# A hybrid mLSTM and attention trunk on one core: halo sums on ScalarE, a ratio with two scalar factors, residual rows loaded as their bank begins

## The chip, the cores and the metric

The kernel runs on one core of one Trainium2 chip. The core has five engines that run side by side, each through its own list of instructions in a fixed order: TensorE (PE in the profile; its weight loads are PEld), VectorE (DVE), ScalarE (ACT), GpSimd (POOL) and SyncE (SP), which here issues all DMAs. They wait for each other by semaphores. The metric is the device time of one execution in microseconds (us), lower is better.

## The reference

Two layers over 2048 rows of width 1024, float32. Each layer normalises the rows, projects them, and splits the columns between two groups of four heads.

```python
h = rmsnorm(x, norm_w)
proj = jnp.einsum('bsd,de->bse', h, w_in)
mq, mk, mv, mi, mf, mz, aq, ak, av, az = jnp.split(proj, idx, axis=-1)
qk = jax.nn.silu(causal_conv(jnp.concatenate([mq, mk], -1), conv_w, conv_b))
...
hm = mlstm_chunkwise(to_heads(mq_c), to_heads(mk_c), to_heads(mv), mi + i_bias, mf + f_bias)
ym = (rmsnorm(hm) + m_skip * mq_c) * jax.nn.silu(mz)
...
ha = diff_attention(qa, ka, av, lam)      # (softmax(q1 k1) - lam * softmax(q2 k2)) v, block-causal
ya = rmsnorm(ha) * (1.0 - lambda_init) * jax.nn.silu(az)
y = jnp.einsum('bse,ed->bsd', jnp.concatenate([ym, ya], -1), w_out)
return x + y
```

`causal_conv` is a depthwise convolution with four taps over time: each output row is a weighted sum of this row and the three before it, plus a bias. Behind the two layers stands one more RMSNorm.

## The kernel before

The rows are cut into four tiles of 512 (t = 0 to 3), each layer goes through its tiles in order, and each tile through four units (u = 0 to 3), one for each pair of an mLSTM head and an attention head: 32 units in all. In a unit TensorE makes six projections of 128 columns (mq, mk, the two gates, and two halves of the rotary q and k) and the value projection, each as products of a high and a low part of both sides; the high parts of the weights are made by ScalarE (`wh`, line 194), the low parts by GpSimd (`wl`, line 196). Beside them run the attention scores (tiles `sc`, `p`), the transposes of the probabilities (`tpa`), which ScalarE copies out as `ath` (line 801) and VectorE completes as `atl` (line 802), the products with the values (`pv`), and the mLSTM recurrence (`ml`).

The order on TensorE is laid down by a planner in the main loop: each task has a time in a list `sched`, tasks of the projections ("P") are chained one behind another, and the side streams ("A" scores, "V" values, "M" mLSTM) are pinned at places of that chain. On the other engines a scheduler of the framework sorts the instructions by the times of its own model of the run, and each engine then works through its list in order. A tile that is allocated anew waits until the last reader of the buffer's earlier content is done; a DMA that waits holds up what stands behind it in SyncE's queue.

The places that the change touches:

- `proj_conv` (line 397), called twice in each unit, for mq and mk, so 64 times. When the projection has landed in a PSUM bank (`mm`), `post` makes the convolution in the SBUF tile `cacc`. Line 406: ScalarE writes tap 3 and the bias. Lines 410 and 412: for each of the other three taps VectorE adds the shifted bank (509 to 511 columns) and, by one small instruction of 1, 2 or 3 columns, what comes from the three last columns of the tile before, the `halo`. Line 414: ScalarE copies the last three columns of the bank into `halo`, for the tile that follows. Lines 394 and 395: the SiLU, a tanh on ScalarE (`th`) and a product on VectorE.
- `ratio` inside `scores` (line 682), 128 times: the two sums of exponentials of a block of 128 queries, `zz`, become the factor by which the second probability map is added to the first. Line 692 takes a reciprocal, line 693 multiplies it by `zz` and by `nl` (minus lambda), a column of 128 equal numbers, as a `scalar_tensor_tensor` with two tensor operands. Line 699 (`chunk`) uses the factor.
- `outproj` (line 880), the output projection, runs in two passes for each tile. The first (`hh` = 0, units 0 and 1) adds the residual rows of the layer's input and stores the sum in DRAM (`xp`); the second (`hh` = 1, units 2 and 3) runs in unit 1 of the next tile, adds the rows of `xp` and stores to `xo`. A pass has eight banks of 256 rows by 256 columns. Lines 915 and 916 load the residual rows `xr` when the bank's last product is issued, line 921 adds, line 925 squares for the next norm (second pass only), line 926 stores. The tag `xr` has two buffers, the tag `x` four. Tag `x` also serves the rows that `prep_t` (line 250) and `prep_x` (line 226) read for the next tile, and the rows of `final` (line 968). Of the last tile the sums stay in SBUF (`rows`), and its second pass loads nothing.

Of the kernel before, what the change touches and what calls it, by code (L numbers as in the profile page):

```python
# [19 lines left out]
P = 128  # L20
# [32 lines left out]
def trunk_kernel(ctx, tc, x, w_ch, w_v0, w_v, w_o, nw, cw, cb, gb, mnw, msk, anw, lam,  # L53
# [83 lines left out]
    def params(l):  # L137
        pr = par[l]
        for nm, src, w in (("cw", cw[l], 32), ("cb", cb[l], 8),
                           ("mnw", mnw[l], NH), ("msk", msk[l], NH), ("anw", anw[l], 1)):  # L140
            t_ = cp.tile([P, w], F32, tag=f"{nm}{l}", name=f"{nm}{l}")
            SY.dma_start(t_, src)
            pr[nm] = t_
        t_ = cp.tile([P, 8], F32, tag=f"gb{l}", name=f"gb{l}")
        SY.dma_start(t_, gb[l].partition_broadcast(P))
        pr["gb"] = t_
        lt = st([P, 4, 64], "tmp", name="lam")
        SY.dma_start(lt, lam[l].partition_broadcast(P))
        lam_init = 0.8 - 0.6 * math.exp(-0.3 * l)
        lp = st([P, 2, 64], "tmp", name="lp")  # L150
        behind(V.tensor_tensor(lp[:, 0], lt[:, 0], lt[:, 1], op=ALU.mult))
        behind(V.tensor_tensor(lp[:, 1], lt[:, 2], lt[:, 3], op=ALU.mult))
        ls = cp.tile([P, 4], F32, tag=f"ls{l}", name=f"ls{l}")
        V.tensor_reduce(out=ls[:, 0:2], in_=lp, axis=AX.X, op=ALU.add)
        A.activation(ls[:, 2:4], ls[:, 0:2], AF.Exp)
        nl = cp.tile([P, 1], F32, tag=f"nl{l}", name=f"nl{l}")

        V.tensor_tensor(nl, ls[:, 3:4], ls[:, 2:3], op=ALU.subtract)
        V.tensor_scalar(out=nl, in0=nl, scalar1=-lam_init, scalar2=None, op0=ALU.add)
        pr["nl"] = nl  # L160

        behind(V.tensor_scalar(out=pr["anw"], in0=pr["anw"], scalar1=(1.0 - lam_init), scalar2=0.5,
                               op0=ALU.mult, op1=ALU.mult))
        behind(V.tensor_scalar(out=pr["mnw"], in0=pr["mnw"], scalar1=0.5, scalar2=None, op0=ALU.mult))
        behind(V.tensor_scalar(out=pr["msk"], in0=pr["msk"], scalar1=0.25, scalar2=None, op0=ALU.mult))

        for h in range(NH):
            hq = cp.tile([P, 2, 3], F32, tag=f"halo{l}{h}", name=f"halo{l}{h}")
            G.memset(hq, 0.0)
            pr["halo"].append(hq)  # L170
        mc = cp.tile([1, NH], F32, tag=f"mc{l}", name=f"mc{l}")
        G.memset(mc, 0.0)
        pr["mc"] = mc
# [220 lines left out]
        A.activation(th, src, AF.Tanh, scale=0.5)  # L394
        V.scalar_tensor_tensor(out=dst, in0=th, scalar=1.0, in1=src, op0=ALU.add, op1=ALU.mult)

    def proj_conv(l, u, qk, H, X):

        pr = par[l]

        def post(ps):
            halo = pr["halo"][u]
            ch = qk * NH + u
            w = lambda j: pr["cw"][:, ch * 4 + j:ch * 4 + j + 1]
            acc = st([P, T], "tmp", name="cacc")
            A.activation(acc, ps, AF.Identity, scale=w(3), bias=pr["cb"][:, ch:ch + 1])  # L406
            for j in (2, 1, 0):

                d = 3 - j
                V.scalar_tensor_tensor(out=acc[:, d:], in0=ps[:, 0:T - d], scalar=w(j), in1=acc[:, d:],  # L410
                                       op0=ALU.mult, op1=ALU.add)
                V.scalar_tensor_tensor(out=acc[:, 0:d], in0=halo[:, qk, j:3], scalar=w(j), in1=acc[:, 0:d],
                                       op0=ALU.mult, op1=ALU.add)
            A.activation(halo[:, qk], ps[:, T - 3:T], AF.Copy)
            nm = "mq" if qk == 0 else "mk"
            X[nm] = st([P, T], nm)
            silu2(X[nm], acc)

        return proj_ch(l, u, qk, H, post)
# [244 lines left out]
    def scores(l, t, u, X, pair):  # L664
# [19 lines left out]
        def ratio(qi, cq, r=None):  # L684
            zz = X["zz"]
            qb = 2 * pair + qi
            z_ = V.tensor_reduce(out=zz[:, qb], in_=cq["zc"][:, :, 0:t + 1], axis=AX.X, op=ALU.add)
            if r is not None:
                after(z_, r)

            s_ = cq["s"] = sm(1, "s12")
            V.reciprocal(s_, zz[:, qb, 1:2])
            V.scalar_tensor_tensor(out=s_, in0=s_, scalar=zz[:, qb, 0:1], in1=pr["nl"], op0=ALU.mult, op1=ALU.mult)
            X["aa", pair].append(cq["pc"][0])

        def chunk(qi, cq, kt, r=None):
# [183 lines left out]
    def outproj(l, t, hh, Xs, es=(0, 1, 2, 3), R=None, halves=(0, 1), c=None):  # L880
# [5 lines left out]
        def task(dq, i, e, lo):  # L886
            def f():
                if e == es[0] and not lo:
                    c["ps"] = pst("mm", [P, 2, 256])
                if (dq, e // 2) not in c["w"]:  # L890
                    c["w"][dq, e // 2] = load_w(w_o[l, hh, dq, e // 2], 512)
                j = e % 2
# [11 lines left out]
                if lo and e == es[-1]:  # L904
# [7 lines left out]
                    if R is not None and hh == 1:  # L912
                        V.tensor_tensor(R[i, dq], c["ps"], R[i, dq], op=ALU.add)  # L913
                        return
                    xr = st([P, 2, 256], "xr")
                    SY.dma_start(xr, src[rows, cs].rearrange("(b p) c -> p b c", p=P))
                    if R is not None:
                        R[i, dq] = st([P, 2, 256], "hth", name="rows")
                        V.tensor_tensor(R[i, dq], c["ps"], xr, op=ALU.add)
# [121 lines left out]
    for k in range(-1, N + 1):  # L1041
# [22 lines left out]
        if cur:  # L1064
# [5 lines left out]
            att += total(q0) + total(q1) + 1.1 * len(v0)  # L1070
            if u == 2 and s < last:
                at(xc, lambda s=s: rs0.__setitem__(s + 1, prep_x((s + 1) // n_t, (s + 1) % n_t)))
            segs.append((0.0, proj_conv(l, u, 0, H, X) + proj_conv(l, u, 1, H, X)))
            if u == 1 and s > 0:
                pl, pt_ = divmod(s - 1, n_t)
                segs.append((fin_t[k - 2] + 6.0, outproj(pl, pt_, 1, Xs[k - 3:k - 1])))
# [173 lines left out]
```

## Time and profile before

| what | value |
|---|---|
| times of the runs | 2815.98, 2825.23 and 2827.08 us (median 2825.23 us) |
| the profiled execution's own time | 2837.46 us |
| its span, first to last instruction | 2835.5 us |
| TensorE busy | 2671.6 us (94%) |
| VectorE, ScalarE, GpSimd busy | 1862.6, 1649.2, 1433.4 us |

The span is what the profiler saw of one execution; the difference of 1.96 us to its own time lies around the first and the last instruction. Busy time is the time in which an engine had an instruction in work; an engine that waits for a semaphore isn't busy. Since TensorE is busy for 94% of the span, its idle time, and what ended each piece of it, is what to look for; an instruction on another engine matters by what TensorE waits for behind it. A wait is put down to the instruction whose semaphore came last. The clock column (PEclk) is the granted TensorE clock as a share of its full speed; 0.50 is 1.2 GHz and 1.00 is 2.4 GHz.

### The profile page before, as it was taken

The numbers are of one execution on the slowest core, as the hardware profiler recorded it, in microseconds if no ns is written. First come the engines' busy times: TensorE is split into PE (matmuls) and PEld (weight loads), VectorE is DVE, ScalarE is ACT, GpSimd is POOL, SyncE is SP. The second block draws the span as 40 slices with busy tenths as digits, with TensorE's granted clock in tenths as the row PEclk, the third lists the DMA queues.
The fourth block names the chain that finished last, engine by engine and source line by source line (L and its number), as shares of the span: only waits on it lengthen the run. The fifth ranks groups of instructions, "written<-read, shape, count | busy, mean of one in ns | idle before, by whom it ended". The sixth has DMA issues, their size and how long they took to land. (4 is left out here: it accounts for less than half of the span.)

```text
span 2835.5 us, 49306 instructions
## 1 busy us (share of the span) xinstructions
PE 2671.6 (94%) x16692; PEld 2371.3 (84%) x16692; DVE 1862.6 (66%) x4890; ACT 1649.2 (58%) x4413; POOL 1433.4 (51%) x1190
## 2 busy tenths in 40 slices
PE   7999899989999999999999999999999999998997
PEld 6898788888888888888888888888888888887887
DVE  5556565775767767567755566567667676776776
ACT  5555465565656556665555555555566555665665
POOL 5565655545454354344445656555554544445425
PEclk9999999999999999999999999999999999999999
DMA  6645555464544544434445455654557444464333
GB/s 203 174 131 157 169 167 149 140 200 150 167 144 128 173 127 127 131 108 139 147 142 177 141 169 154 198 188 137 159 145 231 141 138 154 116 192 145 100 104 119
DMA packets 249789, 431.02 MB, mean 152 GB/s; under 512 B 30400, under 2 KB 106688, under 8 KB 249536
## 3 DMA queue, kind: packets, MB, share of 16 engines
q1 hardware_dynamic: 249536, 427.87, 50.0%
q8 instruction: 132, 2.16, 0.3%
q14 instruction: 121, 0.99, 0.1%
HBM read 314.38 MB, written 63.05 MB: 133 GB/s over the span
## 5 line engine op out<-in xcount | busy, mean ns | idle before, releaser
L196 POOL TENSOR_TENSOR wl<-wr,wh 128x512 fp32r<-128x512 f32 (+1 forms) x684 | 907.6, 1332 | 1070.4 <-PE mm L106 461.7
L194 ACT ACTIVATE wh<-wr 128x512 fp32r<-128x512 f32 (+1 forms) x684 | 428.1, 628 | 414.2 <-PE mm L106 223.5
L106 PE MATMUL mm<-hth,wh 128*128 128x512 f32 x1536 | 619.7, 403 | 0.4 <-ACT vaug L347 0.4
L106 PE MATMUL mm<-htl,wh 128*128 128x512 f32 x1536 | 610.3, 397 | 0.0
L735 DVE TENSOR_SCALAR_CACHE_REDUCE p<-sc 128x512 f32<-128x512 f32 (+3 forms) x640 | 384.7, 606 | 141.7 <-PE sc L106 116.8
L679 ACT ACTIVATE p<-p,nm 128x512 f32<-128x512 f32 (+3 forms) x640 | 413.8, 649 | 97.6 <-DVE nm L675 86.9
L106 PE MATMUL mm<-hth,wl 128*128 128x512 f32 x1536 | 438.8, 400 | 0.0
L106 PEld LDWEIGHTS mm<-hth,wh 128*128 128x128 f32 x1536 | 291.2, 190 | 60.2 <-ACT vaug L347 1.2
L106 PEld LDWEIGHTS mm<-htl,wh 128*128 128x128 f32 x1536 | 291.0, 189 | 56.8
L106 PEld LDWEIGHTS mm<-hth,wl 128*128 128x128 f32 x1536 | 284.1, 190 | 60.2
L699 DVE SCALAR_TENSOR_TENSOR p<-p,s 128x512 f32<-128x512 f32 (+2 forms) x320 | 284.9, 901 | 1.8
L106 PE MATMUL mm<-wh,hth 128*128 128x256 f32 (+1 forms) x1024 | 268.2, 291 | 16.9 <-DVE gt L349 6.0
L802 DVE TENSOR_TENSOR atl<-tpa,ath 128x512 fp32r<-128x512 f32 x288 | 197.1, 684 | 120.4 <-ACT ath L801 119.4
L106 PE MATMUL mm<-wh,htl 128*128 128x256 f32 (+1 forms) x1024 | 264.2, 288 | 0.0
L106 PE MATMUL sc<-kp,q 128*128 128x512 f32 x768 | 246.2, 406 | 5.5 <-DVE p L735 5.4
L801 ACT ACTIVATE ath<-tpa 128x512 fp32r<-128x512 f32 x288 | 170.1, 591 | 139.7 <-PE tpa L109 134.2
L106 PEld LDWEIGHTS mm<-wh,hth 128*128 128x128 f32 x1024 | 198.4, 194 | 22.3 <-issue 9.0
L106 PEld LDWEIGHTS mm<-wh,htl 128*128 128x128 f32 x1024 | 198.3, 194 | 2.5
L109 PE MATMUL tpa<-ident,p 128*128 128x128 f32 x1088 | 186.1, 276 | 15.1 <-DVE tpa L794 8.7
L410 DVE SCALAR_TENSOR_TENSOR cacc<-mm,cw,cacc 128x511 f32<-128x511 f32 (+2 forms) x192 | 141.6, 737 | 66.5 <-ACT cacc L406 64.7
L106 PE MATMUL pv<-ath,vp 128*128 128x256 f32 x768 | 178.9, 287 | 1.1 <-ACT ath L801 1.1
L106 PE MATMUL mm<-wl,hth 128*128 128x256 f32 (+1 forms) x1024 | 166.8, 292 | 0.4 <-POOL wl L196 0.4
(211 smaller groups left out, 5685.1 us busy)
## 6 DMA issues: line engine op xcount, KB each, us to landing
wr<-in_w_ch_dram SPq DMA_DIRECT2D x384, 256.0 KB, 2.7
wr<-in_w_o_dram SPq DMA_DIRECT2D x140, 256.0 KB, 2.9
q<-ab SPq DMA_DIRECT2D x256, 128.0 KB, 2.4
vp<-vd SPq DMA_DIRECT2D x48, 512.0 KB, 4.6
wr<-in_w_v_dram SPq DMA_DIRECT2D x96, 256.0 KB, 3.7
kp<-kd SPq DMA_DIRECT2D x48, 512.0 KB, 3.8
wr<-in_w_v_dram SPq DMA_DIRECT2D x64, 264.0 KB, 3.0
kc<-ab SPq DMA_DIRECT2D x256, 64.0 KB, 2.0
```

What stands on the lines that cost most here:

```text
L106: pin(PE.matmul(o, l, r, start=start, stop=stop, skip_group_check=True))
L109: pin(PE.transpose(o, i, ident[:n, :n]))
L194: A.activation(wh[:, :n], wr[:, :n], AF.Copy)
L196: G.tensor_tensor(wl[:, :n], wr[:, :n], f32(wh[:, :n]), op=ALU.subtract)
L410: V.scalar_tensor_tensor(out=acc[:, d:], in0=ps[:, 0:T - d], scalar=w(j), in1=acc[:, d:], op0=ALU.mult, op1=ALU.add)
L679: A.activation(pp[:, :w], pp[:, :w], AF.Exp, bias=nm[:, m:m + 1], accum_out=zc[:, m, kt:kt + 1])
L699: d_ = V.scalar_tensor_tensor(out=pc[0][kt][:, :w], in0=pc[1][kt][:, :w], scalar=cq["s"][:, 0:1], in1=pc[0][kt][:, :w], op0=ALU.mult, op1= ...
L735: ev = V.tensor_scalar(out=pp[:, :w], in0=ps[:, :w], scalar1=0.125, scalar2=None, op0=ALU.mult, op1=ALU.max, accum_out=c["mx"][:, m, kt:kt ...
L801: A.activation(ah, p2, AF.Copy)
L802: lo_ = V.tensor_tensor(al, p2, f32(ah), op=ALU.subtract)
```

## The change

Three edits. (1) The halo tile no longer holds three columns of the bank but the finished sums that the three first rows of the next tile need: it has a second slot, so that one can be read while the other is written (`was` and `left`), and one tile per unit serves both layers. VectorE's three small instructions per convolution become one addition of three columns, left out in the first tile of a layer; ScalarE's copy becomes one scaled copy and three instructions of one column each that add to it, left out in the last tile. (2) Line 693 of before becomes a `tensor_scalar` whose two factors are columns read as scalars. (3) The load of the residual rows is called as the bank's first product is issued, and in the second pass it takes the tag `x`.

```diff
-            hq = cp.tile([P, 2, 3], F32, tag=f"halo{l}{h}", name=f"halo{l}{h}")
-            G.memset(hq, 0.0)
+            hq = cp.tile([P, 2, 2, 3], F32, tag=f"halo{h}", name=f"halo{l}{h}")
...
-    def proj_conv(l, u, qk, H, X):
+    def proj_conv(l, t, u, qk, H, X):
...
         def post(ps):
-            halo = pr["halo"][u]
             ch = qk * NH + u
             w = lambda j: pr["cw"][:, ch * 4 + j:ch * 4 + j + 1]
+            was, left = [pr["halo"][u][:, qk, i] for i in (t % 2, 1 - t % 2)]
...
                 V.scalar_tensor_tensor(out=acc[:, d:], in0=ps[:, 0:T - d], scalar=w(j), in1=acc[:, d:],
                                        op0=ALU.mult, op1=ALU.add)
-                V.scalar_tensor_tensor(out=acc[:, 0:d], in0=halo[:, qk, j:3], scalar=w(j), in1=acc[:, 0:d],
-                                       op0=ALU.mult, op1=ALU.add)
-            A.activation(halo[:, qk], ps[:, T - 3:T], AF.Copy)
+            if t > 0:
+                V.tensor_tensor(acc[:, 0:3], acc[:, 0:3], was, op=ALU.add)
+            if t < n_t - 1:
+
+                e = ps[:, T - 3:T]
+                A.activation(left, e, AF.Copy, scale=w(0))
+                for j in (1, 2):
+                    for i in range(3 - j):
+                        A.activation(left[:, i:i + 1], e[:, i + j:i + j + 1], AF.Identity, scale=w(j), bias=left[:, i:i + 1])
...
-            V.scalar_tensor_tensor(out=s_, in0=s_, scalar=zz[:, qb, 0:1], in1=pr["nl"], op0=ALU.mult, op1=ALU.mult)
+            V.tensor_scalar(out=s_, in0=s_, scalar1=zz[:, qb, 0:1], scalar2=pr["nl"][:, 0:1], op0=ALU.mult, op1=ALU.mult)
...
                 if e == es[0] and not lo:
                     c["ps"] = pst("mm", [P, 2, 256])
+                    if not (es == (3,) or R is not None and hh == 1):
+                        rows, cs = slice(i * 256, (i + 1) * 256), slice(dq * 256, (dq + 1) * 256)
+                        c["xr"] = st([P, 2, 256], "xr" if hh == 0 else "x")
+                        SY.dma_start(c["xr"], src[rows, cs].rearrange("(b p) c -> p b c", p=P))
...
-                    xr = st([P, 2, 256], "xr")
-                    SY.dma_start(xr, src[rows, cs].rearrange("(b p) c -> p b c", p=P))
+                    xr = c["xr"]
```

In the changed program VectorE has 48 of the three-column additions (now line 412) where it had 192 halo instructions, and ScalarE 48 scaled copies (now line 416) and 144 one-column instructions (now line 419) where it had 64 copies.

The first place is ScalarE's list at one convolution (layer 0, second tile, unit 1, mq). `halo_293` before and `halo_292` now are the halo tile of that unit, `cacc` the convolution, `th` the tanh of it, `ath` the transposed probabilities. Before:

```order
L406 ACTIVATE cacc<-mm,cb_267,cw_265 128x512
L451 ACTIVATE ab<-t_4648 128x512
L596 ACTIVATE hs<-ml 128x129
L814 ACTIVATE ot<-pv 128x256
L600 ACTIVATE mjunk,mss<-hs 128x128
L801 ACTIVATE ath<-tpa 128x512
L194 ACTIVATE wh<-wr 128x512
L414 ACTIVATE halo_293<-mm 128x3
L394 ACTIVATE th<-cacc 128x512
```

Now:

```order
L405 ACTIVATE cacc<-mm,cb_267,cw_265 128x512
L591 ACTIVATE kw<-ml,cols 128x128
L456 ACTIVATE ab<-t_4642 128x512
L819 ACTIVATE ot<-pv 128x256
L806 ACTIVATE ath<-tpa 128x512
L193 ACTIVATE wh<-wr 128x512
L416 ACTIVATE halo_292<-mm,cw_265 128x3
L393 ACTIVATE th<-cacc 128x512
L419 ACTIVATE halo_292<-mm,halo_292,cw_265 128x1 x3
```

The scaled copy stands where the copy stood, in front of the tanh; it waits for VectorE's third tap, where the copy waited for the last halo instruction. The three one-column instructions stand behind the tanh, the first and the third with a wait for a write by ScalarE itself.

The second place is VectorE's list at the same convolution. `atl` is the completed transposed probabilities, `C` the mLSTM state, `den` and `st` the mLSTM's own. Before:

```order
L410 SCALAR_TENSOR_TENSOR cacc<-mm,cw_265,cacc 128x511
L412 SCALAR_TENSOR_TENSOR cacc<-halo_293,cw_265,cacc 128x1
L410 SCALAR_TENSOR_TENSOR cacc<-mm,cw_265,cacc 128x510
L412 SCALAR_TENSOR_TENSOR cacc<-halo_293,cw_265,cacc 128x2
L410 SCALAR_TENSOR_TENSOR cacc<-mm,cw_265,cacc 128x509
L597 SCALAR_TENSOR_TENSOR C_559<-C_559,dec,ml 128x129
L412 SCALAR_TENSOR_TENSOR cacc<-halo_293,cw_265,cacc 128x3
L607 SCALAR_TENSOR_TENSOR den<-hs 128x4
```

Now:

```order
L807 TENSOR_TENSOR atl<-tpa,ath 128x512
L409 SCALAR_TENSOR_TENSOR cacc<-mm,cw_265,cacc 128x511
L589 TENSOR_TENSOR st<-ml,bc 128x128
L409 SCALAR_TENSOR_TENSOR cacc<-mm,cw_265,cacc 128x510
L409 SCALAR_TENSOR_TENSOR cacc<-mm,cw_265,cacc 128x509
L412 TENSOR_TENSOR cacc<-cacc,halo_292 128x3
L807 TENSOR_TENSOR atl<-tpa,ath 128x512
```

Of six instructions of a convolution four are left, and the addition of the halo is the last of them.

The third place is SyncE's queue in the second pass of layer 0's first tile. `xp` is the DRAM tensor that the first pass wrote, `xo` the one that the second writes, `wr` the raw weights. Before:

```order
L926 DMA xo_0_89<-xr 128x2x256
L192 DMA wr<-in_w_o_dram 128x512
L460 DMA kd_1_1_4681<-kc 128x1024
L192 DMA wr<-in_w_o_dram 128x512
L916 DMA xr<-xp_0_81 128x2x256
L658 DMA vp<-vd_3_0_2549 128x1024
L926 DMA xo_0_89<-xr 128x2x256
L192 DMA wr<-in_w_o_dram 128x512 x2
L916 DMA xr<-xp_0_81 128x2x256
```

Now:

```order
L934 DMA xo_0_89<-x 128x2x256
L191 DMA wr<-in_w_o_dram 128x512
L465 DMA kd_1_1_4675<-kc 128x1024
L191 DMA wr<-in_w_o_dram 128x512
L898 DMA x<-xp_0_81 128x2x256
L563 DMA bc<-bw_1_4056 128x2x512
L663 DMA vp<-vd_3_0_2541 128x1024
L934 DMA xo_0_89<-x 128x2x256
L191 DMA wr<-in_w_o_dram 128x512 x2
```

The row `x<-xp` in the second piece is the load of the fifth bank, where the row `xr<-xp` at the same distance behind the first store was the load of the third: the loads of four banks, not of two, now stand ahead of the pass, already in the first pass's stretch of the queue. In the first pass the loads stand where they stood, each behind the store of two banks earlier, since the tag there still has two buffers.

## Rows read from the trace of the kernel before

**Rows 1.** Page, busy time of each engine and share of the span

```profile
PE 2671.6 (94%) x16692; PEld 2371.3 (84%) x16692; DVE 1862.6 (66%) x4890; ACT 1649.2 (58%) x4413; POOL 1433.4 (51%) x1190
```

**Rows 2.** Windows: stretch, length; PE, PEld, DVE, ACT, POOL busy; PEclk; DMA

```profile
32.00:2800.00 2768.00, 2634.27 (x16449) 2338.28 (x16450) 1827.25 (x4807) 1611.24 (x4314) 1396.44 (x1133) 0.98 0.50 151
```

**Rows 3.** Waits of TensorE, 32 to 2800 us: waiter, waited for; us, times, longest

```profile
PE pv L106 <- DVE atl L802: 35.2, 34, 4.6
PE ml L109 <- ACT hs L617: 10.5, 7, 4.7
PE sc L106 <- DVE p L735: 10.2, 15, 1.2
PE ml L106 <- ACT kw L586: 10.1, 9, 2.1
PE pv L106 <- ACT ath L801: 8.6, 9, 2.7
...
PE mm L106 <- DVE xr L921: 6.2, 5, 2.9
...
PE tpa L109 <- DVE s L692: 5.3, 2, 3.2
```

**Rows 4.** VectorE by form: count, busy us, mean ns, idle before

```profile
L693 DVE SCALAR_TENSOR_TENSOR s<-s,zz,nl 128x1 f32<-128x1 f32 x128 | 45.8, 358 | 2.1
...
L412 DVE SCALAR_TENSOR_TENSOR cacc<-halo,cw,cacc 128x1 f32<-128x1 f32 x64 | 38.4, 600 | 0.0
...
L412 DVE SCALAR_TENSOR_TENSOR cacc<-halo,cw,cacc 128x2 f32<-128x2 f32 x64 | 32.8, 512 | 0.0
...
L412 DVE SCALAR_TENSOR_TENSOR cacc<-halo,cw,cacc 128x3 f32<-128x3 f32 x64 | 28.1, 438 | 0.0
...
L835 DVE TENSOR_TENSOR ar<-zz 128x4 f32<-128x4 f32 x31 | 10.7, 346 | 0.0
```

**Rows 5.** Lines 693 and 212: shortest, median, longest duration in ns

```profile
L693 DVE SCALAR_TENSOR_TENSOR s<-s,zz,nl x128: 124/220/1325, 80.8 to 2775.1; 128x1 f32<-128x1 f32 x128
L212 DVE TENSOR_SCALAR xrs<-xrs x16: 145/154/156, 5.6 to 628.6; 128x1 f32<-128x1 f32 x16
```

**Rows 6.** Timeline around one convolution: start, duration [idle before, released by]

```profile
1102.14 1.42 DVE L412 SCALAR_TENSOR_TENSOR cacc<-halo,cw,cacc 128x1 f32<-128x1 f32 x1
1102.24 1.30 POOL L196 TENSOR_TENSOR wl<-wr,wh 128x512 fp32r<-128x512 f32 x1
...
1104.26 0.57 ACT L801 ACTIVATE ath<-tpa 128x512 fp32r<-128x512 f32 x1
...
1105.43 1.26 POOL L196 TENSOR_TENSOR wl<-wr,wh 128x512 fp32r<-128x512 f32 x1 [1.88 <-ACT halo L414]
1105.44 1.26 DVE L693 SCALAR_TENSOR_TENSOR s<-s,zz,nl 128x1 f32<-128x1 f32 x1
...
1106.63 0.68 DVE L802 TENSOR_TENSOR atl<-tpa,ath 128x512 fp32r<-128x512 f32 x1
...
1107.36 0.58 PE L106 MATMUL pv<-atl,vc 128*128 128x256 f32 x1 [2.09 <-DVE atl L802]
```

**Rows 7.** Windows of TensorE behind that wait

```profile
1109.00:1111.00 2.00, 2.00 (x7) 0.50 0.63 143
```

**Rows 8.** Windows: 42 stretches of 8 us and more behind line 406, summed

```profile
sum 527.00, PE 506.68 PEld 424.55 DVE 428.74 ACT 291.63 POOL 326.82; mean PE 12.06 PEld 10.11 DVE 10.21 ACT 6.94 POOL 7.78
```

**Rows 9.** ScalarE by form, as rows 4

```profile
L406 ACT ACTIVATE cacc<-mm,cb,cw 128x512 f32<-128x512 f32 x64 | 49.1, 767 | 7.6 <-PE mm L106 7.4
...
L394 ACT ACTIVATE th<-mm 128x512 f32<-128x512 f32 x64 | 37.8, 590 | 14.5 <-PE mm L106 14.3
...
L414 ACT ACTIVATE halo<-mm 128x3 f32<-128x3 f32 x64 | 10.8, 169 | 85.0 <-DVE cacc L412 84.8
```

**Rows 10.** Waits of all engines, as rows 3

```profile
DVE xr L921 <- DMA xr<-xp: 28.1, 12, 4.4
```

**Rows 11.** Windows: the seven stretches of the second pass, summed

```profile
sum 255.00, PE 247.92 PEld 236.63 DVE 173.31 ACT 170.48 POOL 88.26; mean PE 35.42 PEld 33.80 DVE 24.76 ACT 24.35 POOL 12.61
```

More of the change, by code (lines that the diff above doesn't have):

```diff
@@ L1072, in trunk_kernel @@
                 at(xc, lambda s=s: rs0.__setitem__(s + 1, prep_x((s + 1) // n_t, (s + 1) % n_t)))
-            segs.append((0.0, proj_conv(l, u, 0, H, X) + proj_conv(l, u, 1, H, X)))
+            segs.append((0.0, proj_conv(l, t, u, 0, H, X) + proj_conv(l, t, u, 1, H, X)))
             if u == 1 and s > 0:
```

## The prediction

> **What bounds the kernel now.** I read the page's busy times first. TensorE works for 2671.6 of 2835.5 us, the next engine, VectorE, for 1862.6 [rows 1]. So only TensorE's idle time can be won or lost. The windows say where it is: between 32 and 2800 us TensorE is busy for 2634.27 of 2768.00 us, which leaves 133.7 us idle [rows 2]; the rest lies at the two ends, which the change hardly touches. The waits say what ends it. The largest group, 35.2 us in 34 pieces, is TensorE standing before `pv` until VectorE has made `atl`; 10.2 us are waits for `p`, 5.3 us for the instruction just ahead of the ratio, and 10.5, 10.1 and 8.6 us are waits for ScalarE (`hs`, `kw`, `ath`) [rows 3]. No single wait is large (76 pieces in these six groups), and each is there because VectorE or ScalarE was still working through its list. A change on those engines is worth what it takes off these waits, not the time that it takes off the engine.
>
> One more thing makes a wait dearer than it looks. Behind the wait that ended at 1107.36 us [rows 6], TensorE ran from 1109 to 1111 us without a gap at a granted clock of 0.50, the 1.2 GHz level [rows 7]: those 2 us hold 1 us of work at full speed.
>
> **Edit 1, VectorE's side.** It removes 192 small instructions: 38.4 + 32.8 + 28.1 = 99.3 us [rows 4], 1.55 us for each of 64 convolutions. It adds 48 additions of 128x3. The nearest row is an addition of 128x4 from two SBUF tensors, 346 ns on average [rows 4]: 48 x 0.346 = 16.6 us. From below I bound it by a one-source instruction of one column, 0.15 us [rows 5], so 7 us, from above by the dearest halo form, 0.60 us [rows 4], so 29 us. VectorE is relieved by about 83 us (70 to 92).
>
> Why a 128x1 instruction takes 600 ns is seen in the timeline: one took 1.42 us, while GpSimd's `wl` ran from 1102.24 to 1103.54 us, and line 693 took 1.26 us while the next `wl` ran for 1.26 us from 1105.43 us [rows 6]. Both have two tensor inputs in SBUF. Behind them stood `atl`, started at 1106.63 us though its input `ath` was done at 1104.83 us, and behind `atl` TensorE for 2.09 us. With the edits that list is shorter by 1.42 and two times some 0.2 us of halo work and by 1.1 us of ratio, less 0.35 us for the addition: `atl` could start when `ath` is there, 1.8 us earlier, and of the 2.09 us some 0.3 would be left. This is one of the best places, not a typical one.
>
> What it is worth over all: the stretches behind the 64 convolutions (42 of them, since the two of a unit often touch) are 527.00 us long and TensorE is busy in them for 506.68 us [rows 8]. So 20.3 us of idle time can go at most, and part of it ends on ScalarE. I take half, 10 us. What is late next in those stretches is `ath` on ScalarE, or TensorE itself.
>
> **Edit 1, ScalarE's side.** 64 copies of 169 ns go (10.8 us). A scale and a bias read from columns cost 767 - 590 = 177 ns, by the same shape with and without them [rows 9]; one of them I take at 88 ns. The scaled copy then takes 0.26 us and each one-column instruction 0.35 us: 0.26 + 3 x 0.35 = 1.31 us, 48 times, 63 us. ScalarE's work grows by 52 us (22 us if the columns cost nothing, 85 us if an instruction takes 0.5 us, because each adds to what the one before has written; no row shows that wait). Against this stands the wait of the old copy for VectorE's last halo instruction, 84.8 us [rows 9]; the new one waits for the third tap only, 1.55 us earlier, and 16 convolutions have none. So ScalarE comes out about even, but its work stands closer to `ath` and `kw`, for which TensorE waits already [rows 3]. I charge 2 us (0 to 24, the upper end worked out below).
>
> **Edit 2.** Line 693 takes 358 ns on average, 124 at the shortest and 1325 at the longest [rows 4, 5]. A `tensor_scalar` of the same 128x1 took 145 to 156 ns in all its 16 instances [rows 5]. By that row 128 x (358 - 152) = 26 us of VectorE's time go. The other bound is nothing, if the new form is held up by GpSimd as the old one was. On the path: 51 waits of TensorE end at `atl`, `p` or `s` [rows 3]; if a ratio stood ahead of every one, 0.2 us each, 10 us. It stands ahead of a minority, so I take 3 us.
>
> Here the Trainium skill speaks against the edit. Its page "SBUF — State Buffer", section "Who interferes with whom", says that a VectorE instruction with two SBUF inputs contends with a GpSimd instruction that reads SBUF, and that `tensor_scalar` can contend too when it runs in a two-port mode; whoever starts first holds the shared ports for its whole instruction. The first half agrees with the 1.42 and 1.26 us above [rows 6]. By the second half the edit would save nothing and the sum below would be 3 us smaller; the 16 instances of the one-column `tensor_scalar` without a long one [rows 5] speak against it here.
>
> **Edit 3.** In the first pass nothing moves: the loads already stand as early as two buffers allow. In the second pass VectorE waited 28.1 us, 12 times, for the loads [rows 10], which themselves wait in SyncE's queue for the stores of two banks earlier. With four buffers VectorE's wait should go. But in the seven stretches of the second pass TensorE is busy for 247.92 of 255.00 us [rows 11], so 7.1 us is all there is, and in both passes together it stood for 6.2 us behind the addition of the rows [rows 3]. I take 1 us (0 to 7). The loads of `prep_x` for the next tile, which share the tag, now come behind the second pass; they have a unit's time until they are used, so I cost them at nothing. If that cover is gone, the transposes of the next tile wait.
>
> **The sum.** 10 + 3 + 1 - 2 = 12 us of waits. With some of the longer waits a stretch at the 1.2 GHz level goes too; I take three of them at 1 us [rows 7]. Total 15 us. The profiled execution's own time is 2837.46 us, so its like would be 2822.5 us; that execution lay 12.2 us above the median of the runs, so I predict 2837.5 - 15 - 12.2 = 2810 us, 0.5% under the 2825.2 us. Its own range, from 7 to 25 us of gain, is 2800 to 2818 us.
>
> **Rivals.** (a) The relief is hidden. TensorE's order is fixed, and where one engine is earlier, another ends the same wait: behind `atl` stands `ath`, behind that TensorE's own transposes. For it speaks that the convolution stretches are idle for 3.9% (20.3 of 527), hardly less tight than the 4.8% overall (133.7 of 2768); against it the list of [rows 6], where nothing else was late. Gain 3 us: 2822 us (2815 to 2830).
>
> (b) ScalarE takes the wait's place. The scaled copy still waits for VectorE's third tap, and all that stands behind it on ScalarE waits with it; then come three instructions that each need the one before, and the PSUM bank is free only behind the last. If in each of 48 convolutions this puts an `ath`, `kw` or `wh` that TensorE is about to need 0.5 us later, TensorE loses 24 us, and some 4 us at the lower clock. Against a VectorE relief of 15 us the time is 2825 + 28 - 15 = 2838 us. It decides from about 0.3 us per convolution on. For it: 29.2 us of waits for ScalarE already [rows 3]. Against it: ScalarE is busy for 58% only [rows 1], and the old copy stood and waited at the same place.
>
> (c) More goes than I count: 26 us of ratio and 83 us of halo are 6% of VectorE's work, and they went into every wait for `atl`; if half of the 50.7 us of waits for VectorE's `atl`, `p` and `s` [rows 3] goes, with 5 us of lower clock, the gain is 30 us: 2795 us.
>
> (d) The `tensor_scalar` is held up like the old form (the page above): edit 2 gives nothing, 2813 us.
>
> That an edit does not do what it says can be told of the third alone: its first half changes no load's place.
>
> **How the numbers follow.** Chances: forecast 0.42, (a) 0.22, (b) 0.15, (c) 0.15, (d) 0.06. About 0.5% (14 us) can be told from no change, so faster means below 2811 us and slower above 2839 us. The forecast's range lies across the first line: 0.28 below, 0.14 above. (a) and most of (d) are no change, (c) is faster, of (b) 0.13 is slower. Faster 0.28 + 0.15 + 0.02 = 0.45; same 0.14 + 0.22 + 0.04 + 0.02 = 0.42; slower 0.13. The range runs from 2790 (beyond (c)) to 2836 us (nearly at (b)).
>
> **What would show it.** Edit 1: the halo lines' 99.3 us on VectorE become some 17, and ScalarE's halo lines rise from 10.8 to some 63 us. Edit 2: a mean near 155 ns and no instance above 1 us; means near 350 say (d). Edit 3: no wait of VectorE for `x<-xp`. On the path: TensorE's busy time stays at 2671 us and its idle time between 32 and 2800 us falls from 133.7 to about 120 us; waits for `atl` fall below 30 us. If the waits for `ath`, `kw` and `wh` grow by more than those fall, (b) was right. If VectorE's time falls as said and TensorE's idle time does not, (a).

## The result and the profile after

The changed kernel takes 2795.24 us (median of 4 runs, 2788.99 to 2797.66) against 2825.85 us for the kernel before on the same chip (4 runs, 2815.98 to 2827.08). The ratio is 0.9895, with a 95% interval of 0.9875 to 0.9915: 30.6 us, or 1.05%, faster. The prediction was 2810 us. Its sign was right, its gain of 15 us half of what came. The profiled execution took 2792.97 us, 2.3 us below its median, while that of before lay 12.2 us above; of the 44.5 us between the two profiles some 14 are therefore chance, and the traces are compared with that in mind.

The busy times of the changed kernel (answers to [rows 1]):

```profile
PE 2656.9 (95%) x16692; PEld 2359.0 (85%) x16692; DVE 1796.1 (64%) x4746; ACT 1688.5 (60%) x4541; POOL 1439.6 (52%) x1182
```

TensorE has the same 16692 instructions and is busy for 14.7 us less, at a mean granted clock of 0.988 where the profile of before has 0.981. The clock need not be all of it: one of the versions below (rows, nudged up) was busy for 2680.2 us at 0.982. Its idle time over the whole span falls from 163.9 us (2835.5 - 2671.6) to 134.4 us (2791.3 - 2656.9). VectorE is relieved of 66.5 us where 109 were forecast (83 + 26), ScalarE takes on 39.3 us where 52 were forecast.

The window between the two ends (columns as in [rows 2]):

```profile
32.00:2756.00 2724.00, 2619.60 (x16450) 2326.38 (x16451) 1760.71 (x4662) 1649.11 (x4438) 1402.89 (x1132) 0.99 0.52 153
```

TensorE is idle for 104.4 us in it, where it was 133.7 us [rows 2]; about 120 us were forecast. The waits in it, columns as in [rows 3]:

```profile
PE pv L106 <- DVE atl L807: 23.6, 32, 3.0
PE pv L106 <- ACT ath L806: 12.7, 14, 2.1
PE sc L106 <- DVE p L740: 11.8, 16, 1.7
PE mm L106 <- DVE gt L348: 10.5, 5, 2.7
PE ml L109 <- ACT hs L622: 7.3, 3, 5.2
PE ml L106 <- ACT kw L591: 6.9, 6, 1.8
...
PE tpa L109 <- DVE s L697: 3.7, 2, 2.0
...
PE mm L106 <- DVE xr L929: 0.3, 1, 0.3
```

The wait for `atl` is 11.6 us shorter and below the 30 us that were asked of it; those for `hs`, `kw` and `s` fall by 3.2, 3.2 and 1.6 us. Waits for `ath` (8.6 to 12.7), `p` (10.2 to 11.8) and the gates' columns `gt` (6.0 to 10.5) grow: part of the place of VectorE's `atl` is taken by other waits. The wait behind the addition of the rows, 6.2 us before, is 0.3 us.

VectorE's groups by form (columns as in [rows 4]), and the shortest, median and longest instance of two of them (as in [rows 5]):

```profile
L929 DVE TENSOR_TENSOR x<-mm,x 128x512 f32<-128x512 f32 x56 | 38.4, 685 | 15.9 <-PE mm L106 13.9 <-DMA x<-in_x_dram 1.1 <-DMA x<-xp 0.2
L698 DVE TENSOR_SCALAR s<-s,zz,nl 128x1 f32<-128x1 f32 x128 | 34.2, 267 | 2.1
...
L412 DVE TENSOR_TENSOR cacc<-cacc,halo 128x3 f32<-128x3 f32 x48 | 22.0, 458 | 0.0
```

```profile
L698 DVE TENSOR_SCALAR s<-s,zz,nl x128: 158/272/276, 78.5 to 2730.9; 128x1 f32<-128x1 f32 x128
L412 DVE TENSOR_TENSOR cacc<-cacc,halo x48: 140/294/1299, 327.7 to 2677.3; 128x3 f32<-128x3 f32 x48
```

No instance of the ratio is held up any more (longest 276 ns, where 1325 ns was seen), but it takes 267 ns on average (median 272), not the 152 ns of the one-column instruction with constants; so it saves 128 x (358 - 267) = 11.6 us, not 26. The halo's 99.3 us became 22.0. VectorE's 28.1 us wait for the residual rows in the second pass [rows 10] is down to 0.2 us (`x<-xp` in the first row).

ScalarE's groups (answers to [rows 9]):

```profile
L419 ACT ACTIVATE halo<-mm,halo,cw 128x1 f32<-128x1 f32 x144 | 42.9, 345 | 0.2
L393 ACT ACTIVATE th<-cacc 128x512 f32<-128x512 f32 x64 | 40.1, 626 | 16.3 <-DVE cacc L412 16.0
L416 ACT ACTIVATE halo<-mm,cw 128x3 f32<-128x3 f32 x48 | 12.3, 257 | 15.5 <-DVE cacc L409 15.2
```

257 and 345 ns stand against the forecast 0.26 and 0.35 us. The wait of 84.8 us in front of the old copy is now 15.2 us in front of the scaled copy and 16.0 us in front of the tanh.

Last the two sums over stretches: 38 stretches of 8 us and more behind line 405 (answer to [rows 8]), then the second pass (answer to [rows 11]):

```profile
sum 501.00, PE 491.40 PEld 413.48 DVE 373.11 ACT 327.92 POOL 337.58; mean PE 12.93 PEld 10.88 DVE 9.82 ACT 8.63 POOL 8.88
...
sum 242.00, PE 235.27 PEld 225.05 DVE 155.23 ACT 170.29 POOL 86.20; mean PE 33.61 PEld 32.15 DVE 22.18 ACT 24.33 POOL 12.31
```

Behind the convolutions TensorE idles for 9.6 us, where it was 20.3: 10.7 us less, for a forecast of 10. In the second pass it idles for 6.7 us, where it was 7.1: as good as nothing, for a forecast of 1. So the two places that these sums show came out about as priced, and yet the window as a whole lost 29.3 us of idle time. Outside of the convolutions' stretches it fell from 113.4 (133.7 - 20.3) to 94.8 us (104.4 - 9.6): 18.6 us that the prediction had put nowhere.

### The profile page after: what moved, and what is told of

The parts are those of the page before. It is cut to its first block, busy times and chain, and to the rows that moved or that the text cites. A ratio compares the mean times of both kernels' runs of the same rounds, so it can differ in the third digit from the quotient of the medians.

```text
span 2791.3 us, 49265 instructions
## 1 busy us (share of the span) xinstructions
PE 2656.9 (95%) x16692; PEld 2359.0 (85%) x16692; DVE 1796.1 (64%) x4746; ACT 1688.5 (60%) x4541; POOL 1439.6 (52%) x1182
## 5 line engine op out<-in xcount | busy, mean ns | idle before, releaser
L106 PEld LDWEIGHTS mm<-hth,wh 128*128 128x128 f32 x1536 | 291.2, 190 | 59.3 <-ACT vaug L346 0.9
L106 PE MATMUL mm<-wh,hth 128*128 128x256 f32 (+1 forms) x1024 | 264.9, 289 | 10.9 <-DVE gt L348 10.5
```

Source lines behind the costliest of these rows:

```text
L106: pin(PE.matmul(o, l, r, start=start, stop=stop, skip_group_check=True))
```

## The experiments

Three edits, alone and in pairs, in up to three orders of the work. The order is written by a planner in the kernel from a table of numbers, so an edit also reshuffles the program. To tell an edit's worth from such luck, one of these numbers is changed by about a hundredth: `MS`, the distance at which the planner sets the blocks of the mLSTM behind each other. That leaves every instruction what it is and only moves some of them ("nudged").

The table has all versions. Time and ratio: median of the timed runs, and against the kernel before timed beside it on the same chip. Clock: each timed run lists its span and its mean granted clock; the means over the runs are given of span x (1 - clock), what the 1.2 GHz level took off, and of span x clock, the rest. The clock is a mean over the whole span, so idle time at the lower level counts as lost to it too; the split is a way of counting. Idle: TensorE's idle time in the profiled execution (span less busy), behind the convolutions as above and everywhere else. The last column adds up TensorE's waits for `atl`, `hs` and `kw` in that execution. A profiled execution is a single one; those of the rows alone lay 15.5 and 12.8 us above their version's median.

| version | us | ratio (95%) | span x clock | lost to clock | idle behind conv. | idle elsewhere | atl + hs + kw |
|---|---|---|---|---|---|---|---|
| before (80 runs) | 2825.9 to 2828.6 | 1 | 2784.1 | 40.8 | 20.3 | 143.6 | 55.8 |
| before, nudged up | 2833.57 | 1.0031 (1.0015-1.0047) | 2788.6 | 43.9 | 24.0 | 143.3 | 64.8 |
| before, nudged down | 2821.08 | 0.9978 (0.9966-0.9989) | 2776.7 | 41.3 | 20.0 | 134.5 | 44.3 |
| halo | 2828.57 | 0.9994 (0.9979-1.0009) | 2778.1 | 48.0 | 8.6 | 146.9 | 56.8 |
| halo, nudged up | 2820.90 | 0.9981 (0.9969-0.9992) | 2770.6 | 48.6 | 10.5 | 132.7 | 45.3 |
| ratio | 2826.17 | 0.9990 (0.9977-1.0003) | 2779.1 | 45.0 | 17.9 | 139.1 | 52.2 |
| rows | 2830.77 | 1.0005 (0.9987-1.0023) | 2788.2 | 40.1 | 20.1 | 149.5 | 59.9 |
| rows, nudged up | 2828.74 | 1.0014 (0.9996-1.0031) | 2785.9 | 42.0 | 19.2 | 140.1 | 59.3 |
| halo + ratio | 2812.42 | 0.9941 (0.9919-0.9962) | 2766.3 | 44.5 | 12.3 | 134.1 | 51.5 |
| ratio + rows | 2814.49 | 0.9959 (0.9943-0.9974) | 2776.4 | 37.1 | 19.9 | 125.0 | 45.4 |
| halo + rows | 2797.32 | 0.9891 (0.9872-0.9911) | 2760.7 | 34.5 | 7.6 | 130.0 | 36.9 |
| halo + rows, nudged up | 2796.69 | 0.9887 (0.9870-0.9903) | 2756.4 | 36.9 | 10.4 | 125.9 | 32.7 |
| all three (after) | 2795.24 | 0.9895 (0.9875-0.9915) | 2759.0 | 33.5 | 9.6 | 124.8 | 38.2 |
| all three, nudged up | 2789.14 | 0.9869 (0.9850-0.9888) | 2756.9 | 31.2 | 12.3 | 117.2 | 34.2 |

**Each edit alone.** Edit 1 alone (`halo_only`):

```diff
-                V.scalar_tensor_tensor(out=acc[:, 0:d], in0=halo[:, qk, j:3], scalar=w(j), in1=acc[:, 0:d],
-                                       op0=ALU.mult, op1=ALU.add)
-            A.activation(halo[:, qk], ps[:, T - 3:T], AF.Copy)
+            if t > 0:
+                V.tensor_tensor(acc[:, 0:3], acc[:, 0:3], was, op=ALU.add)
+            if t < n_t - 1:
...
+                A.activation(left, e, AF.Copy, scale=w(0))
```

> The kernel before with edit 1 alone (halo sums on ScalarE). Theory A, what counts is VectorE's relief and each edit brings its own part: VectorE's busy time falls by about 75 us, the time by 14 to 22 us, so about 2808 us. Theory B, the gain of 31 us comes from the residual rows (SyncE's queue and VectorE's waits for rows): within 5 us of before. Theory C, any new order of the lists moves the time by as much: no relation to the edit, anything between -30 and +30 us, and the single edits don't add up to 31 us.

Measured: 0.9994, no gain. Edit 2 alone (`ratio_only`):

```diff
-            V.scalar_tensor_tensor(out=s_, in0=s_, scalar=zz[:, qb, 0:1], in1=pr["nl"], op0=ALU.mult, op1=ALU.mult)
+            V.tensor_scalar(out=s_, in0=s_, scalar1=zz[:, qb, 0:1], scalar2=pr["nl"][:, 0:1], op0=ALU.mult, op1=ALU.mult)
```

> The kernel before with edit 2 alone (ratio as tensor_scalar). Theory A: VectorE is relieved by 11 to 12 us (358 to about 267 ns, 128 times), the time falls by 2 to 6 us, about 2822 us. Theory B: no change (within 3 us). Theory C: no relation, up to 30 us either way.

Measured: 0.9990, no gain that its interval shows. Edit 3 alone (`rows_only`):

```diff
+                        c["xr"] = st([P, 2, 256], "xr" if hh == 0 else "x")
+                        SY.dma_start(c["xr"], src[rows, cs].rearrange("(b p) c -> p b c", p=P))
...
-                    xr = st([P, 2, 256], "xr")
-                    SY.dma_start(xr, src[rows, cs].rearrange("(b p) c -> p b c", p=P))
+                    xr = c["xr"]
```

> The kernel before with edit 3 alone (residual rows loaded at the bank's begin, tag x in the second pass). Theory A: VectorE's 28 us of waits for rows go, but TensorE hardly stood there, so the time falls by 0 to 5 us, about 2823 us. Theory B: this edit carries the gain, 20 us or more, below 2806 us. Theory C: no relation, up to 30 us either way.

Measured: 1.0005. Edits 1 and 2 together, without the third (`halo_ratio`):

```diff
+                V.tensor_tensor(acc[:, 0:3], acc[:, 0:3], was, op=ALU.add)
...
+            V.tensor_scalar(out=s_, in0=s_, scalar1=zz[:, qb, 0:1], scalar2=pr["nl"][:, 0:1], op0=ALU.mult, op1=ALU.mult)
```

> Edits 1 and 2 without edit 3: the changed kernel with the residual rows loaded as before. Theory A: nearly all of the gain, 18 to 28 us under before, 2798 to 2808 us. Theory B: within 8 us of before. Theory C: not the sum of the two single edits within 8 us.

Measured: 0.9941, 16 us. So no edit carries the change, and the three alone add up to nothing: 0.9994 x 0.9990 x 1.0005 = 0.9989, where all three together give 0.9895. The pair stays under the 18 to 28 us of theory A (every edit brings its own part), and the theory that the rows bring all of it (B) fell. Whether a part of each edit was hidden by the luck of its order is taken up below.

**How much is luck of the order?** The kernel before with that one number changed (`before_nudged`):

```diff
-MS = 4.2
+MS = 4.25
```

> The kernel before with one number of the planner changed (MS from 4.2 to 4.25, the spacing of the mLSTM steps): same instructions, order of the lists shifted by about as much as edit 2 shifts it (side streams on TensorE move by 0.2 to 0.7 projection products on average). Theory C (the order alone moves the time by as much as the change did): 10 us or more from before, either way. Theory D (the edits work together: while one long list is left on VectorE, it ends the same waits): within 8 us of before.

Measured: 1.0031, 7.7 us slower. The same for the changed kernel (`after_nudged`):

```diff
-MS = 4.2
+MS = 4.25
```

> The changed kernel with the same nudge of the planner (MS 4.25). Theory C: the gain was luck of this order, so much of the 31 us goes, 2805 us or more. Theory D: it stays within 8 us of the changed kernel, 2789 to 2805 us.

Measured: 0.9869, the lowest time of all versions, though its interval overlaps with that of the changed kernel (0.9875 to 0.9915). And the kernel before, nudged to the other side (`before_nudged2`):

```diff
-MS = 4.2
+MS = 4.15
```

> The kernel before with the planner's MS at 4.15: a third order of the same instructions. Theory E (each edit has its own effect, by the eight kernels about -18 us for the halo, -14 for the rows, -9 for the ratio, and each order of the lists adds some 8 us of luck of either sign, of which the kernel before had a good draw): 2 to 12 us slower than before, 2828 to 2838 us. Theory D (single edits are worth nothing, pairs are): within 4 us of before.

Measured: 0.9978. A reshuffle by itself moves the time by -0.2 to +0.3%, that is -6 to +8 us. That is as much as each edit alone shows, so such a single ratio tells little; it is far from 31 us. Luck alone (theory C) fell: 10 us or more were asked of it in the nudged kernel before, and much of the gain should have gone in the nudged changed one.

**Which pair?** Edits 1 and 3 (`halo_rows`):

```diff
+                V.tensor_tensor(acc[:, 0:3], acc[:, 0:3], was, op=ALU.add)
...
+                        c["xr"] = st([P, 2, 256], "xr" if hh == 0 else "x")
```

> Edits 1 and 3 without edit 2. The single edits brought 0 to 3 us each, edits 1 and 2 together 16 us, all three 31 us. Theory D: the pair is worth more than its parts, 8 to 18 us under before. Theory C: no relation, and as likely slower than before. If edit 2 (the factor without a wait for GpSimd) is what has to be there, within 5 us of before.

Measured: 0.9891, the whole gain of the change and more than the 8 to 18 us that theory D gave it. Edits 2 and 3 (`ratio_rows`):

```diff
+            V.tensor_scalar(out=s_, in0=s_, scalar1=zz[:, qb, 0:1], scalar2=pr["nl"][:, 0:1], op0=ALU.mult, op1=ALU.mult)
...
+                        c["xr"] = st([P, 2, 256], "xr" if hh == 0 else "x")
```

> Edits 2 and 3 without edit 1. Theory D: worth more than its parts, 6 to 14 us under before, less than with edit 1, since the 79 us of halo instructions stay on VectorE. Theory C: no relation. If the halo edit is what has to be there, within 5 us of before.

Measured: 0.9959. Every pair came out worth more than its parts, as theory D has it, but the two pairs with the ratio ran in one order only. The ratio adds nothing that can be told once the other two are in (0.9891 against 0.9895, and nudged 0.9887 against 0.9869 with intervals that overlap).

**Is that itself luck?** The other explanation was that each edit has a worth of its own and the single runs had bad orders (theory E). So the two edits were run again, alone and together, in another order. Edit 1 (`halo_nudged`):

```diff
-MS = 4.2
+MS = 4.25
...
+                V.tensor_tensor(acc[:, 0:3], acc[:, 0:3], was, op=ALU.add)
```

> Edit 1 alone, MS 4.25. Theory E: 9 us under before and up to 8 us of luck, 2809 to 2825 us, most likely faster than edit 1 alone in the first order. Theory D: at before's time like edit 1 alone, within 4 us.

Measured: 0.9981. Edit 3 (`rows_nudged`):

```diff
-MS = 4.2
+MS = 4.25
...
+                        c["xr"] = st([P, 2, 256], "xr" if hh == 0 else "x")
```

> Edit 3 alone, MS 4.25. Theory E: 5 us under before and up to 8 us of luck, 2813 to 2829 us. Theory D: at before's time, within 4 us.

Measured: 1.0014. Both (`halo_rows_nudged`):

```diff
-MS = 4.2
+MS = 4.25
...
+                V.tensor_tensor(acc[:, 0:3], acc[:, 0:3], was, op=ALU.add)
...
+                        c["xr"] = st([P, 2, 256], "xr" if hh == 0 else "x")
```

> Edits 1 and 3, MS 4.25. Theory E: the pair's 31 us had some 8 us of luck in it, so 23 us under before and up to 8 us either way, 2795 to 2811 us. Theory D: the pair's gain is the edits' own, 2792 to 2802 us.

Measured: 0.9887. Against the kernel before as it stands, the edits alone give next to nothing in both orders and together some 31 us. Against its own base, the nudged kernel before (1.0031), the halo is worth 0.9981 / 1.0031 = 0.9950 (14 us) and the rows 0.9983 (5 us), which multiply to 0.9933; the pair has 0.9887 / 1.0031 = 0.9856 (41 us). So the pair is worth 31 us more than its parts in the first order and 22 us more in the second.

That does not exclude theory E. Of what was expected, E's ranges held for three of these four kernels (2820.90, 2828.74 and 2796.69 us) and failed for the kernel before at 4.15, which came out faster and not slower. Theory D's held for two; it failed for that kernel and for the nudged halo, each 6 us under before where 4 were allowed. For D speak the two differences, and the last column of the table: `atl`, `hs` and `kw` make TensorE wait 32.7 to 38.2 us in all four versions that have both edits, and 44.3 to 64.8 us in the ten others. Against it, each difference is made of four kernels with some 7 us of luck each (the spread of the three orders of before), which leaves it, by estimate, some 14 us of luck. That the pair is worth more than its parts is likely, but not certain.

**Where the pair's gain lies.** The table's means over the orders (three without the edits, two each with) split it. Of span x clock the halo takes off 8.8 us (2783.1 to 2774.3), the rows add 3.9, both together take off 24.6 (2758.5): 20 us more than the sum of the two. Of the time lost to the clock the halo adds 6.3 us (42.0 to 48.3), the rows take off 0.9, both together 6.3: 12 us more. By this count two thirds of what only the pair brings is waits and one third is time at the lower clock. The halo alone is the plainest case: it frees some 9 us and gives 6 back at 1.2 GHz. The 9 us are less than the orders of before differ by (2776.7 to 2788.6); the 6 us are not (40.8 to 43.9 without an edit, 48.0 and 48.6 with the halo).

The split of the idle time says where the waits are. Behind the convolutions the halo edit does its work in every version: seven versions without it idle there for 17.9 to 24.0 us, seven with it for 7.6 to 12.3 us, means of 20.2 and 10.2. It is everywhere else that the single edits bring nothing (132.7 to 149.5 us, as in the three orders of before, 134.5 to 143.6) and pairs and the whole change do (117.2 to 134.1), though these ranges touch.

Waits of TensorE over the whole execution show three that differ. Edit 1 alone:

```profile
PE pv L106 <- DVE atl L807: 30.1, 30, 4.7
PE ml L109 <- ACT hs L622: 16.2, 6, 5.9
...
PE ml L106 <- ACT kw L591: 10.5, 9, 2.1
```

Edit 3 alone:

```profile
PE pv L106 <- DVE atl L802: 30.7, 36, 2.2
PE ml L109 <- ACT hs L617: 15.5, 6, 4.7
PE ml L106 <- ACT kw L586: 13.7, 9, 2.7
```

Edits 1 and 3:

```profile
PE pv L106 <- DVE atl L807: 23.9, 27, 4.7
...
PE ml L109 <- ACT hs L622: 6.5, 2, 5.1
PE ml L106 <- ACT kw L591: 6.5, 6, 1.8
```

Either edit alone takes some 5 us off the 35.2 us for `atl` and puts as much on the 10.5 us for `hs` [rows 3]; with both, `atl`, `hs` and `kw` all fall. For a single edit this is no more than an order moves: the three orders of before have 29.0 to 37.9 us for `atl` and 6.2 to 15.0 us for `hs`. One piece, in the last tile of layer 0 (window 1088 to 1182 us), edit 1 alone and then edits 1 and 3:

```profile
PE ml L109 <- ACT hs L622: 4.8, 2, 4.5
PE tpa L109 <- POOL ar L843: 3.2, 1, 3.2
```

```profile
PE tpa L109 <- POOL ar L843: 2.0, 1, 2.0
PE sc L106 <- DVE p L740: 2.0, 1, 2.0
```

With edit 1 alone a wait of 4.5 us for `hs` stands there; with the rows edit too it is gone. Other profiles do not tie this to the pair. In the same window the waits for `hs` are 5.0 us with edit 1 nudged, 4.6 us with edit 3 and none with the pair nudged, but 1.0 us, 4.4 us and none in the three orders of before and 1.0 us in halo + ratio. That a wait freed by one edit is taken by the next in line until the other edit frees that too is argued, not shown.

**Why VectorE gained less than it lost in work.** With edit 1 alone the halo's 99.3 us became 20.5 us, 78.8 less, but VectorE's busy time fell by 28.7 us only (1862.6 to 1833.9). The same forms on VectorE in the kernel before, then with edit 1 alone:

```profile
L395 DVE SCALAR_TENSOR_TENSOR mq<-th,cacc 128x512 f32<-128x512 f32 x32 | 25.5, 797 | 12.0 <-ACT th L394 12.0
L395 DVE SCALAR_TENSOR_TENSOR mk<-th,cacc 128x512 f32<-128x512 f32 x32 | 22.4, 699 | 11.7 <-ACT th L394 11.6
...
L699 DVE SCALAR_TENSOR_TENSOR p<-p,s 128x128 f32<-128x128 f32 x32 | 13.7, 427 | 0.0
```

```profile
L698 DVE SCALAR_TENSOR_TENSOR s<-s,zz,nl 128x1 f32<-128x1 f32 x128 | 50.4, 394 | 1.9
...
L394 DVE SCALAR_TENSOR_TENSOR mq<-th,cacc 128x512 f32<-128x512 f32 x32 | 30.0, 939 | 10.7 <-ACT th L393 10.7
L394 DVE SCALAR_TENSOR_TENSOR mk<-th,cacc 128x512 f32<-128x512 f32 x32 | 27.5, 861 | 12.7 <-ACT th L393 12.5
...
L412 DVE TENSOR_TENSOR cacc<-cacc,halo 128x3 f32<-128x3 f32 x48 | 20.5, 428 | 0.0
L704 DVE SCALAR_TENSOR_TENSOR p<-p,s 128x128 f32<-128x128 f32 x32 | 17.2, 537 | 0.0
```

Four groups that the edit does not touch became longer by 4.6 (the ratio, 45.8 before), 4.5, 5.1 and 3.5 us. All have two tensor inputs in SBUF, as the old halo instructions had. For the first three it holds in the other versions too: `mq` takes 26.7 to 30.1 us with the halo edit and 25.1 to 25.5 us without, `mk` 24.3 to 28.0 and 22.0 to 24.3, the ratio in its old form 50.4 to 55.1 and 43.4 to 48.7. The last moves as much with the order (13.7 to 17.8 us without the edit). What became of such an instruction is seen in the timeline of edit 1 alone (start, duration, engine):

```profile
1496.02 2.54 POOL L457 TENSOR_TENSOR ab<-t,ab 128x512 fp32r<-128x512 f32 x2
1497.75 2.62 DVE L394 SCALAR_TENSOR_TENSOR mq<-th,cacc 128x512 f32<-128x512 f32 x1 [0.85 <-ACT th L393]
1498.53 1.29 POOL L195 TENSOR_TENSOR wl<-wr,wh 128x512 fp32r<-128x512 f32 x1
```

`mq` takes 2.62 us where its shortest instance takes 0.67, and ends 0.55 us behind GpSimd's `wl`. It looks as if the small halo instructions were in part only the ones that stood and waited for GpSimd; with them gone the next one does. The four groups make 17.7 of the 50 us that are missing; neighbouring records overlap a little, so that removing 144 instructions also frees less than their listed time, and the rest is open. This pair of profiles is also the extreme one: in the five other pairs that differ by the halo edit, VectorE's busy time falls by 41.2 to 49.9 us. With the ratio edit added to the halo (1793.8 us busy in halo + ratio) VectorE falls by 40.1 us more, and added to halo + rows (1823.5) by 27.4, where the ratio alone brings 18.9 (1843.7): this fits the same hand-over, read from the other side.

## Why the prediction was half right

- *What bounds the kernel*: right. TensorE's idle time (29.5 us less) and its busy time (14.7 us less) make the whole of the 44.2 us between the two spans.
- *Edit 1 on VectorE, 83 us*: the halo's lines gave 77.3 us, near the 83; the addition takes 458 ns, not 346, because it too stands behind GpSimd (all eight instances above 0.9 us, the longest 1299 ns, end within 0.05 us of a GpSimd instruction that ran beside them). On the engine it was less, by the hand-over above.
- *Edit 1 on the path, 10 us behind the convolutions*: right in size and place, 10.7 us in the pair of profiles and 10.0 in the means of seven versions each. The half that was taken of the 20.3 us was a guess, so the size is in part luck.
- *Edit 1 on ScalarE*: 257 and 345 ns as worked out, 55.2 us busy in all where 63 were forecast. The charge of 2 us and rival (b): ScalarE's waits grew for `ath` by 4.1 us and fell for `hs` and `kw` by 6.4, so on the whole nothing was lost.
- *Edit 2, 3 us*: the shape of its rival (d) fell (longest instance 276 ns). The Trainium skill, "SBUF — State Buffer", section "Who interferes with whom", says that `tensor_scalar` can contend with GpSimd too, in a two-port mode. This one shows no such wait in 128 instances. But it takes 267 ns where the row with constants took 152; no run tells whether the two scalars read from columns are all of that. With both other edits in, it is worth nothing that can be told.
- *Edit 3, 1 us*: VectorE's wait went and the second pass gained 0.4 us, as said. But TensorE's wait behind the addition of the rows, of whose 6.2 us only 0.4 lay in the second pass's stretches, is 0.3 to 2.0 us in all seven versions with this edit and 4.3 to 6.4 us in the seven without: some 4 us, where 1 was taken. What was costed at nothing, the loads for the next tile that now come behind the second pass, did move idle time about. Three stretches of TensorE, before and then after (columns as in [rows 2]):

```profile
415.00:479.00 64.00, 63.33 (x445) 58.68 (x444) 33.12 (x108) 41.54 (x127) 33.13 (x28) 1.00 0.60 183
564.00:648.00 84.00, 73.61 (x525) 69.02 (x524) 57.00 (x153) 48.86 (x129) 35.56 (x32) 0.94 0.62 194
741.00:810.00 69.00, 68.11 (x505) 64.23 (x504) 46.87 (x125) 45.40 (x135) 32.03 (x26) 1.00 0.53 161
```

```profile
415.00:479.00 64.00, 59.48 (x366) 52.93 (x365) 33.68 (x96) 38.34 (x119) 34.09 (x31) 0.97 0.55 166
564.00:648.00 84.00, 80.41 (x562) 73.16 (x562) 53.90 (x152) 46.67 (x117) 41.47 (x34) 1.00 0.56 175
741.00:810.00 69.00, 63.64 (x409) 55.62 (x408) 38.52 (x119) 43.07 (x131) 27.99 (x26) 0.98 0.54 168
```

  In the middle stretch, where the squares of the next tile's rows stood before, idle time fell from 10.4 to 3.6 us; in the other two, where they stand now, it rose from 0.7 to 4.5 and from 0.9 to 5.4 us. The stretches do not hold the same work (445 and 366 instructions in the first), but the other versions bear it out: in the middle stretch TensorE idles for 9.1 to 13.1 us in all seven without this edit and 3.6 to 4.3 us in all seven with it, in the last for 0.6 to 1.5 and 4.6 to 5.6 us. Net it is nothing: the three together make 12.0 to 14.4 us without it and 11.2 to 14.2 us with it. The transposes of the next tile, named as the risk, do not wait: behind 32 us TensorE has no wait for their rows in either profile.
- *The clock, 3 us*: too small; 7.3 us by the means over the timed runs (40.8, on three chips 38.6 to 43.0, to 33.5). In the two profiles TensorE's busy time, which was to stay at 2671 us, fell by 14.7 us. In the window, PEclk rose from 0.98 to 0.99.
- *The sum*: this is the step that failed. It priced each edit at one place, added the prices and put everything else at nothing. The places were right, but the sum misses the 18.6 us of idle time that went elsewhere, and it has 3 us of clock where 7.3 came. Some 6 of the 18.6 us are the wait behind the rows. The rest is seen in no edit alone. As the experiments have it, likely but not certain, each edit's freed time is then taken by another wait or given back at the lower clock, as rival (a) had it, and the halo and the rows together free what neither frees. Rival (c), "more goes than I count", had the number, 2795 us, but not the reason: the waits for `atl`, `p` and `s` fell by 11.6 us together (50.7 to 39.1), not by half, and the rest came off waits for `kw`, `hs`, the rows and several smaller ones, and off the clock.

What stays open: why the stretches at 1.2 GHz come and go (the mean clock of the kernel before runs from 0.981 to 0.989 over its own 80 runs, so it takes no new order for that), why the halo alone loses more to the clock, and by what chain of waits the halo and the rows need each other.

## What to carry to other kernels

When one engine is busy for 94% and many small waits of several engines hold up the rest, price an edit at its place, but test edits in pairs too: alone they can show nothing and together 1%. Measure first how much a mere reshuffle of the order moves the time (here 0.2 to 0.3%), and run an edit in two orders before its single ratio is believed. Taking away an instruction that stands and waits for a shared resource need not take away all of the wait, if the next one in line needs the same.

## What was not expected of the hardware

- A VectorE `tensor_scalar` of one column took 267 ns on average with two scalars read from columns, never more than 276 ns in 128 instances, and 145 to 156 ns with constants [rows 5].
- VectorE's waits for GpSimd seem to be handed on: 78.8 us of halo instructions less gave 28.7 us less busy time (41.2 to 49.9 us in other pairs of versions), and untouched instructions with two SBUF inputs became 10 to 23% longer (ratio 358 to 394 ns, `mq` 797 to 939, `mk` 699 to 861).
- The same TensorE instructions were busy for 2671.6 us at a mean granted clock of 0.981 in one execution and for 2656.9 us at 0.989 in another, in another order. Over its own 80 runs the kernel before has the same range of clocks, 0.981 to 0.989.
